# Encoder trunk in three-product float32: the feed-forward low halves made by an accumulating transfer, and the first weights loaded chunk by chunk

## The chip, the cores and the metric

The kernel runs on one core of a Trainium2 chip. The time is device microseconds of one execution; several executions are measured and the median is quoted. Beside the times there is the profile of one execution, taken by the hardware profiler; its span runs from the first instruction to the last.

## The reference

The model is an encoder trunk of two layers on 512 tokens of width 1024, all in float32. Each layer mixes tokens in three ways side by side, merges them, and then applies a SwiGLU feed-forward block and a gated per-layer embedding. Cut to what matters here (the three mixers are attention, a convolution and a windowed attention):

```python
for i in range(DEPTH):                                  # DEPTH = 2
    h = rmsnorm(x, norm_mix[i])
    proj = h @ w_in[i]                                  # 1024 -> 7168
    qa, ka, va, glu_in, qc, kc, vc, gates = jnp.split(proj, SPLITS, axis=-1)
    ...
    x = x + merged @ w_o[i]
    h = rmsnorm(x, norm_ffn[i])
    x = x + (jax.nn.silu(h @ w_ffn_gate[i]) * (h @ w_ffn_up[i])) @ w_ffn_down[i]
    h = rmsnorm(x, norm_ple[i])
    x = x + jax.nn.sigmoid(h @ w_ple_gate[i]) * (p[i] @ w_ple_in[i])
return rmsnorm(x, norm_final)
```

The feed-forward width is 2816, so a layer's gate and up weights are 1024 x 2816 each and its down weights 2816 x 1024.

## The kernel before

**Three products for one.** TensorE takes its operands in a shortened float32 format (`F32R`). To keep float32 accuracy every operand is held as two tiles: a high half, which is the value rounded to that format, and a low half, which is what the rounding left, value minus high half. A product is then three matmuls (`mm3`, lines 175 to 177): high weights by high activations, high weights by low activations, low weights by high activations. The low weights are read by the third matmul of each trio.

**How the two halves are made.** `split` (lines 160 to 162) does it with two engines: ScalarE copies the source into the high tile (an `ACTIVATE` at L141), and VectorE subtracts that from the source into the low tile (a `TENSOR_TENSOR` at L155). `weights` (lines 164 to 171) loads one weight tile and splits it: SyncE's queue loads up to 128x1024 values into a raw tile `wr` (512 KB, L169), and the two halves go to `wh` and `wl`. There are three buffers of each of `wr`, `wh` and `wl`. A raw buffer is free for the next load when VectorE has read it; the two others when TensorE's last matmul on them is done. The last instruction of the split is kept in `self.low`, which one stage outside the feed-forward block uses to place background work behind it.

**Queues and order.** TensorE's order is written out by hand. The other engines' orders are made by a scheduler from priorities; `weights` raises the priority of its instructions so that they are issued early. Each engine works through its own list in order. POOL's list before is short: constants, small memsets, and one `pow` for each norm.

**The feed-forward stage** (`ffn`, lines 917 to 958; instructions named `ffn_...`). A layer does it in two halves of 11 blocks of the feed-forward width. For each block, `gemm` makes the gate product and then the up product, each with one 128x1024 weight tile (24 matmuls). The first gate and up of a layer are done as a `pair` (lines 192 to 202): seven of the eight chunks of both, then the last chunk of both, so both weight tiles are held to the end. After 11 blocks the half of the down projection follows: eight outputs, each with one 128x1024 tile and one 128x384 tile (24 and 9 matmuls). Over two layers that is 120 large tiles and 32 small ones. Beside the weights ScalarE does the SiLU and the high half of the gated result, VectorE the scalings by the norm, the multiplications and the low half.

**The opening** (`opening`, lines 307 to 366; instructions named `pre_...` and the first `glu_...`). The first four blocks of 128 output columns (gate and value of the convolution branch) are made together, chunk by chunk over the eight 128-row chunks of the input, while the input and the weights arrive. Ten warm-up matmuls on zeros (`WARM`, L319) come first. The norm's gains lie in a table of parameters `par`: eight columns of it are loaded first on ScalarE's queue, the rest at the fourth chunk. The weights of the four blocks come as separate transfers of 128, 128, 256 and 512 columns for each block. Each input chunk `x` is scaled and split by `operand` (lines 257 to 266: ScalarE makes the high half, VectorE the low one), and its square is added to a running sum by `sumsq`. A small scale computed from the parameters (`lambdas`, L415) is VectorE work that the scheduler may place between these.

Of the kernel before, what the change touches and what calls it, by code (L numbers as in the profile page):

```python
# [11 lines left out]
F32 = mybir.dt.float32  # L12
F32R = mybir.dt.float32r
I32 = mybir.dt.int32
AF = mybir.ActivationFunctionType
ALU = mybir.AluOpType
# [4 lines left out]
P = 128  # L21
# [5 lines left out]
KD = 8  # L27
HA = 4
HC = 8
CB = 512  # L30
# [11 lines left out]
OFF_QA, OFF_KA, OFF_VA, OFF_GLU = 0, 512, 1024, 1536  # L42
# [2 lines left out]

PAR_L = 8 + 8 + 8 + 1 + 4 + 4 + 4 + 4 * CON3W
PAR = L * PAR_L + 8
WARM = 10
BG = dict(glu=2, natten=1, values=3, diff=1, gatec=2, branchc=2, gateb=4, mergea=4, mergea2=2)
FIRST = (["v"] * 4 + ["pt"] * 2 + ["y", "b"], ["y"] * 5 + ["pt"] * 2 + ["b"])  # L50
EARLY = 6
# [8 lines left out]
class Net:  # L60
# [103 lines left out]
    def weights(self, ap, n):  # L164
        with self.tc.high_priority(offset=min(self.w_ahead, self.tc.cur_priority - self.p0)):
            raw = self.sb("wr", [P, 1024])
            hi = self.sb("wh", [P, 1024], F32R)
            lo = self.sb("wl", [P, 1024], F32R)
            self.nc.sync.dma_start(raw[:, :n], ap[:, :n])  # L169
            self.low = self.split(hi[:, :n], lo[:, :n], raw[:, :n])  # L170
        return hi, lo

    def mm3(self, out, wh, wl, ah, al, first, last):
# [133 lines left out]
    def opening(self):  # L307

        nc, a = self.nc, self.a
        self.parts = self.sb("par", [P, PAR], bufs=1)  # L310
        self.small()
        mix = slice(0, KD)
        xc = [t for _ in range(KD // 2) for t in self.parts_of("x", [512], 2)]
        nc.sync.dma_start(xc[0], a["xT"][0])
        nc.scalar.dma_start(self.parts[:, mix], a["par"][:, mix])
        self.consts()
        warm = self.ps("av")
        for _ in range(WARM):
            nc.tensor.matmul(warm, self.zero_r, self.zero_r[:, None, :].to_broadcast([P, 4, P]),  # L319
                             start=True, stop=True)  # L320
        blocks = []
        lows = [t for _ in range(2) for t in self.parts_of("qk", [1024], 2, F32R)]
        raws = {"t": [self.sb("t", [P, P]) for _ in range(4)],
                "a": [self.sb(t, [P, P]) for t in ("a", "a", "a", "kh")],
                "rp": [self.sb("rp", [P, 256]) for _ in range(4)],
                "e": [self.sb("e", [P, 512]) for _ in range(4)]}
        for m in range(4):
            src = a["w_in"][0, (OFF_GLU + (0 if m % 2 else CB)) // P + m // 2]
            blocks.append((src, self.sb("y", [P, 1024], F32R), lows[m],
                           self.ps("sc" if m == 3 else "mm")))  # L330
        self.first = [b[3] for b in blocks]
        h, st = [], []
        self.i, self.phase = 0, "glu"
        for k in range(KD):
            if k > 1:
                nc.sync.dma_start(xc[k], a["xT"][k])
            pieces = {0: (0, P, "t"), 1: (P, 256, "a"), 2: (256, 512, "rp"), 4: (512, 1024, "e")}
            if k == 0:
                nc.scalar.dma_start(raws["t"][0], blocks[0][0][:, 0:P])
            elif k == 1:  # L340
                nc.scalar.dma_start(xc[1], a["xT"][1])
            elif k == 3:
                nc.scalar.dma_start(self.parts[:, KD:], a["par"][:, KD:])
            h.append(self.operand(xc[k], self.par(0, "mix", k), FIRST[0][k]))
            if k in pieces:
                c0, c1, tag = pieces[k]
                for m, (src, wh, wl, _) in enumerate(blocks):
                    raw = raws[tag][m]
                    if k or m:
                        nc.sync.dma_start(raw, src[:, c0:c1])  # L350
                    if k or m:
                        self.split(wh[:, c0:c1], wl[:, c0:c1], raw)
                    else:
                        nc.vector.tensor_copy(wh[:, c0:c1], raw)
                        self.tt(wl[:, c0:c1], raw, wh[:, c0:c1].bitcast(F32), ALU.subtract)
            s = slice(k * P, k * P + P)
            for src, wh, wl, ps in blocks:
                self.mm3(ps, wh[:, s], wl[:, s], *self.halves(h[k]), k == 0, k == KD - 1)
            if k:
                self.sumsq(k - 1, xc[k - 1], st)  # L360
            if k == KD - 1:
                self.sumsq(k, xc[k], st)
                self.main_norm(st[0], (1, 1), xc)
            self.tick()
        self.p0 = self.tc.cur_priority
        return h
# [785 lines left out]
def _blocks(w):  # L1152
    k, m = w.shape[-2:]
    lead = w.shape[:-2]
    n = len(lead)
    w = w.reshape(*lead, k // P, P, m // P, P)
    w = w.transpose(*range(n), n + 2, n + 1, n, n + 3)
    return np.ascontiguousarray(w).reshape(*lead, m // P, P, (k // P) * P)


def _vblocks(w):
    w = w.reshape(L, KD, P, 2, 256).transpose(0, 3, 2, 1, 4)
    return np.ascontiguousarray(w).reshape(L, 2, P, KD * 256)
# [7 lines left out]
def _cols(v):  # L1171
    v = v.reshape(-1, v.shape[-1])
    return v.reshape(v.shape[0], -1, P).transpose(2, 0, 1).reshape(P, -1)


def _token_order():
    t = np.arange(S)
    return (t % GR) * GW + t // GR


def _rope_tables():
    inv = np.float32(1.0) / (10000.0 ** (np.arange(0, 64, 2) / 64)).astype(np.float32)
    ang = np.arange(S, dtype=np.float32)[:, None] * inv[None, :]
    ang = np.concatenate([ang, ang], axis=-1)
    cos, sin = np.cos(ang), np.sin(ang)
    sin[:, :32] = -sin[:, :32]
    n = _token_order()
    return np.ascontiguousarray(
        np.stack([np.concatenate([c[n].T, c[n].T], axis=0) for c in (cos, sin)])).astype(np.float32)


def _bias_tiles(rpb):
    t = np.arange(S)
    w, r = t // GR, t % GR
    cs = np.clip(w - NA_KC // 2, 0, GW - NA_KC)
    out = np.full((L, HC, 4, P, NW), FILL, dtype=rpb.dtype)
    for qt in range(4):
        q = np.arange(qt * P, (qt + 1) * P)
        k = np.arange(NW) + KEY0[qt]
        ro = r[k][None, :] - r[q][:, None] + NA_KR - 1  # L1200
        co = w[k][None, :] - w[q][:, None] + NA_KC - 1
        ok = (w[k][None, :] >= cs[q][:, None]) & (w[k][None, :] < cs[q][:, None] + NA_KC)
        out[:, :, qt] = np.where(ok, rpb[:, :, np.where(ok, ro, 0), np.where(ok, co, 0)],
                                 out[:, :, qt])
    out = out.reshape(L, HC, 2, 2, P, NW).transpose(0, 1, 2, 4, 3, 5)
    return np.ascontiguousarray(out)


def _layout(v):
    n = _token_order()  # L1210
    f = {k: np.asarray(a) for k, a in v.items()}
    w_in = f["w_in"]
    par = []
    for i in range(L):
        par += [_cols(f["norm_mix"][i]), _cols(f["norm_ffn"][i]), _cols(f["norm_ple"][i]),
                _cols(f["subln_g"][i]), _cols(f["conv_b"][i]), _cols(f["cln_g"][i]),
                _cols(f["cln_b"][i]),
                f["conv_w"][i, :, 0, :].reshape(CON3W, 4, P).transpose(2, 1, 0).reshape(P, -1)]
    par.append(_cols(f["norm_final"]))
    lam = np.stack([np.stack([f["lam_q1"], f["lam_q2"]]), np.stack([f["lam_k1"], f["lam_k2"]])])  # L1220
    down = f["w_ffn_down"].reshape(L, 2, HB * P, D)
    return {
        "xT": np.ascontiguousarray(f["x"][0][n].T).reshape(KD, P, S),
        "pT": np.ascontiguousarray(f["p"][:, 0][:, n].transpose(0, 2, 1)).reshape(L, 2, P, S),
        "par": np.ascontiguousarray(np.concatenate(par, axis=1)),
        "lam": np.ascontiguousarray(np.broadcast_to(lam.reshape(1, 2, 2 * L * 64), (P, 2, 2 * L * 64))),
        "rope": _rope_tables(),
        "bias": _bias_tiles(f["rpb"]),
        "w_in": _blocks(w_in),
        "w_va": _vblocks(w_in[:, :, OFF_VA:OFF_VA + 512]),  # L1230
        "w_vc": _wide(w_in[:, :, OFF_VC:OFF_VC + 512]),
        "w_br_a": _blocks(f["w_br_a"]),
        "w_br_b": _blocks(f["w_br_b"]),
        "w_br_c": _blocks(f["w_br_c"]),
        "w_o": _blocks(f["w_o"]),
        "w_fg": _blocks(f["w_ffn_gate"]),
        "w_fu": _blocks(f["w_ffn_up"]),
        "w_fd": _blocks(down),
        "w_pi": _blocks(f["w_ple_in"]),
        "w_pg": _blocks(f["w_ple_gate"]),  # L1240
    }
# [15 lines left out]
```

## Time and profile before

| | |
|---|---|
| median of 3 runs | 1819.57 us (1818.94 to 1822.36) |
| the profiled execution | 1819.71 us |
| its span | 1817.9 us |
| granted TensorE clock, mean | 0.999 |
| feed-forward weights loaded | 44 + 44 + 32 tiles of 512 KB, 32 of 192 KB |
| feed-forward low halves on VectorE | 152 instructions, 164.7 us |
| transfer engines' share over the span | q1, SyncE's queue: 38.3% |

The page of the profile gives busy time of each engine: PE is TensorE's matmuls, PEld its weight loads, DVE is VectorE, ACT ScalarE, POOL GpSimd, SP SyncE, whose queue only issues transfers (SPq). The chain of waits is the work that ended last, followed back from the end. In the groups a line reads: source line, engine, operation, output tile from input tiles, shapes and count, then busy time and mean duration, then the engine's idle time just before and what ended it. In a timeline the first number is the start in us from the span's start and the second the duration; what stands in square brackets is the idle time before and its releaser. A table of windows gives, for a stretch, each engine's busy us and instructions, the granted TensorE clock, the transfer engines' share and GB/s. A DMA issue line gives the count, the KB of one, and the median us from issue to landing.

### The profile page before, as it was taken

The numbers are of one execution on the slowest core, as the hardware profiler recorded it, in microseconds if no ns is written. First come the engines' busy times: TensorE is split into PE (matmuls) and PEld (weight loads), VectorE is DVE, ScalarE is ACT, GpSimd is POOL, SyncE is SP. The second block draws the span as 40 slices with busy tenths as digits, with TensorE's granted clock in tenths as the row PEclk, the third lists the DMA queues.
The fourth block names the chain that finished last, engine by engine and source line by source line (L and its number), as shares of the span: only waits on it lengthen the run. The fifth ranks groups of instructions, "written<-read, shape, count | busy, mean of one in ns | idle before, by whom it ended". The sixth has DMA issues, their size and how long they took to land.

```text
span 1817.9 us, 23237 instructions
## 1 busy us (share of the span) xinstructions
PE 1806.6 (99%) x8628; PEld 1514.5 (83%) x8628; DVE 1188.2 (65%) x1913; ACT 767.2 (42%) x1316; POOL 24.6 (1%) x58
## 2 busy tenths in 40 slices
PE   9999999999999999999999999999999999999998
PEld 7888888888888888888888888888888888888887
DVE  7877888988644434445777788889875443344456
ACT  5577555325332222233535765552353332232344
POOL 0000000000000000000000000000000000000000
PEclk9999999999999999999999999999999999999999
DMA  5665531325422233223446655322362322322232
GB/s 194 194 180 167 157 110 59 105 96 178 138 93 94 81 107 103 103 76 118 149 139 202 168 159 153 92 76 95 107 205 94 104 93 80 118 93 97 80 113 93
DMA packets 91455, 221.10 MB, mean 122 GB/s; under 512 B 12240, under 2 KB 22352, under 8 KB 91344
## 3 DMA queue, kind: packets, MB, share of 16 engines
q1 hardware_dynamic: 90192, 218.09, 38.3%
q8 instruction: 68, 1.11, 0.3%
q10 hardware_dynamic: 1152, 1.55, 0.2%
q14 instruction: 43, 0.35, 0.1%
HBM read 180.79 MB, written 7.34 MB: 103 GB/s over the span
## 4 chain that ended last, share of the span: by engine, by line
PE 96%; ACT 2%; DVE 1%; DMA 1%; issue 0%; SPq 0%; POOLq 0%; DVEq 0%; ACTq 0%
PE ffn_mm L175 13%; PE ffn_mm L176 13%; PE ffn_mm L177 13%; PE mergea_mm L176 2%; PE mergea_mm L175 2%; PE mergea_mm L177 2%; PE diff_sc L793 2%; PE gatec_mm L175 2%; PE gatec_mm L176 2%; PE gatec_mm L177 2%; PE gateb_mm L176 2%; PE gateb_mm L175 2%; PE wo_mm L175 2%; PE gateb_mm L177 2%; PE wo_mm L176 2%; PE wo_mm L177 2%
## 5 line engine op out<-in xcount | busy, mean ns | idle before, releaser
L141 ACT ACTIVATE ffn_wh<-ffn_wr 128x1024 fp32r<-128x1024 f32 (+1 forms) x152 | 144.0, 949 | 513.9 <-issue 383.2
L175 PE MATMUL ffn_mm<-wo_h,ffn_wh 128*128 128x512 f32 x704 | 274.2, 390 | 0.0
L177 PE MATMUL ffn_mm<-wo_h,ffn_wl 128*128 128x512 f32 x704 | 273.9, 389 | 0.0
L176 PE MATMUL ffn_mm<-wo_h,ffn_wh 128*128 128x512 f32 x704 | 273.9, 389 | 0.0
L155 DVE TENSOR_TENSOR ffn_wl<-ffn_wr,ffn_wh 128x1024 fp32r<-128x1024 f32 (+1 forms) x152 | 164.7, 1085 | 129.6 <-ACT ffn_wh L141 129.6
L158 DVE SCALAR_TENSOR_TENSOR conv_z<-glu_z,pre_par,conv_z 128x512 f32<-128x512 f32 x240 | 179.6, 749 | 3.3
L177 PEld LDWEIGHTS ffn_mm<-wo_h,ffn_wl 128*128 128x128 f32 x704 | 132.1, 188 | 27.7
L175 PEld LDWEIGHTS ffn_mm<-wo_h,ffn_wh 128*128 128x128 f32 x704 | 132.1, 188 | 27.3
L176 PEld LDWEIGHTS ffn_mm<-wo_h,ffn_wh 128*128 128x128 f32 x704 | 132.2, 188 | 27.2
L155 DVE TENSOR_TENSOR ffn_t<-ffn_t,ffn_mm 128x512 f32<-128x512 f32 x44 | 30.2, 687 | 114.8 <-PE ffn_mm L177 114.8
L155 DVE TENSOR_TENSOR ffn_t<-ffn_mm,wo_r 128x512 f32<-128x512 f32 x44 | 30.4, 691 | 110.4 <-PE ffn_mm L177 110.4
L141 ACT ACTIVATE mergea_wh<-mergea_wr 128x1024 fp32r<-128x1024 f32 (+1 forms) x32 | 27.1, 846 | 96.8 <-PE mergea_mm L176 79.6
L175 PE MATMUL ffn_mm<-ffn_z,ffn_wh 128*128 128x512 f32 x160 | 62.2, 389 | 0.0
L176 PE MATMUL ffn_mm<-ffn_z,ffn_wh 128*128 128x512 f32 x160 | 62.2, 389 | 0.0
L177 PE MATMUL ffn_mm<-ffn_z,ffn_wl 128*128 128x512 f32 x160 | 62.2, 389 | 0.0
L175 PE MATMUL ffn_mm<-ffn_y,ffn_wh 128*128 128x512 f32 x160 | 62.2, 389 | 0.0
L176 PE MATMUL ffn_mm<-ffn_y,ffn_wh 128*128 128x512 f32 x160 | 62.2, 389 | 0.0
L177 PE MATMUL ffn_mm<-ffn_y,ffn_wl 128*128 128x512 f32 x160 | 62.2, 389 | 0.0
L141 ACT ACTIVATE diff_a<-diff_sc,diff_s 128x512 f32<-128x512 f32 x32 | 22.0, 686 | 61.3 <-DVE diff_s L884 61.3
L884 DVE TENSOR_REDUCE diff_s<-diff_sc 128x1 f32<-128x512 f32 x64 | 42.1, 685 | 3.9 <-PE diff_sc L793 3.7
L141 ACT ACTIVATE natten_wh<-natten_wr 128x1024 fp32r<-128x1024 f32 x24 | 25.4, 1058 | 41.6 <-issue 15.2
L155 DVE TENSOR_TENSOR wo_x<-wo_x,ffn_mm 128x512 f32<-128x512 f32 x32 | 22.0, 687 | 31.5 <-PE ffn_mm L177 31.5
(662 smaller groups left out, 4564.9 us busy)
## 6 DMA issues: line engine op xcount, KB each, us to landing
ffn_wr<-w_fg SPq DMA_DIRECT2D x44, 512.0 KB, 3.2
ffn_wr<-w_fu SPq DMA_DIRECT2D x44, 512.0 KB, 3.2
ffn_wr<-w_fd SPq DMA_DIRECT2D x32, 512.0 KB, 3.5
natten_wr<-w_in SPq DMA_DIRECT2D x16, 512.0 KB, 3.6
natten_b<-bias SPq DMA_DIRECT2D x32, 256.0 KB, 3.6
diff_wr<-w_in SPq DMA_DIRECT2D x16, 512.0 KB, 3.8
gatec_wr<-w_in SPq DMA_DIRECT2D x16, 512.0 KB, 3.6
gateb_wr<-w_in SPq DMA_DIRECT2D x16, 512.0 KB, 3.2
```

The source lines that it names most:

```text
L141: i = self.nc.scalar.activation(out, in_, func, **kw)
L155: return self.nc.vector.tensor_tensor(out, a, b, op)
L158: return self.nc.vector.scalar_tensor_tensor(out, a, s, b, op0, op1)
L175: mm(out, wh, ah, start=first, stop=False)
L176: mm(out, wh, al, start=False, stop=False)
L177: mm(out, wl, ah, start=False, stop=last)
L793: self.nc.tensor.matmul(out, st4[:, u, qs], st[:, ks], start=n == 0, stop=n == 1)
L884: nc.vector.tensor_reduce(out=m[:, u:u + 1], in_=sc, op=ALU.max, axis=AX.X, negate=True)
```

## The change

In the feed-forward stage the low half of a weight tile is no longer made by VectorE. ScalarE writes the high half as before and then the negative of the rounded source into the low tile (a second `ACTIVATE`, with scale -1 into an `F32R` tile); then a transfer issued by GpSimd reads the raw tile and adds it onto the low tile, SBUF to SBUF. All other stages keep `split`.

In the opening the host lays the weights of the first four blocks out chunk by chunk (`w_0`: for each 128-row chunk, the 512 columns of the four blocks side by side), and puts the eight norm gains and the first block's first 128 columns into one array `head`. `head` is loaded first on SyncE's queue, the first chunk of x on ScalarE's; then for each chunk one x and one weight transfer of 256 KB on SyncE's queue, and the whole parameter table after the fourth chunk. Each chunk's weights are split in one piece (the first 128 columns of the first chunk by VectorE alone). `WARM` goes from 10 to 8.

```diff
-WARM = 10
+WARM = 8
...
             self.nc.sync.dma_start(raw[:, :n], ap[:, :n])
-            self.low = self.split(hi[:, :n], lo[:, :n], raw[:, :n])
+            if self.phase == "ffn":
+                self.act(hi[:, :n], raw[:, :n], AF.Copy)
+                self.act(lo[:, :n], raw[:, :n], AF.Copy, scale=-1.0)
+                self.low = self.nc.gpsimd.dma_start(lo[:, :n].bitcast(F32), raw[:, :n], accum_op=ALU.add)
+            else:
+                self.low = self.split(hi[:, :n], lo[:, :n], raw[:, :n])
...
-        nc.sync.dma_start(xc[0], a["xT"][0])
-        nc.scalar.dma_start(self.parts[:, mix], a["par"][:, mix])
+        raws = [self.sb(tag, [P, 512]) for tag in ("rp", "e") for _ in range(4)]
+        head = self.sb("a", [P, KD + P])
+        nc.sync.dma_start(head, a["head"])
+        nc.scalar.dma_start(xc[0], a["xT"][0])
+        nc.sync.dma_start(raws[0], a["w_0"][0])
...
         for k in range(KD):
-            if k > 1:
+            if k:
                 nc.sync.dma_start(xc[k], a["xT"][k])
...
+                nc.sync.dma_start(raws[k], a["w_0"][k])
+            if k == 3:
+                nc.sync.dma_start(self.parts, a["par"])
+            hi, lo = his[k], los[k]
             if k == 0:
...
-            h.append(self.operand(xc[k], self.par(0, "mix", k), FIRST[0][k]))
...
+                first = head[:, KD:]
+                nc.vector.tensor_copy(hi[:, :P], first)
+                self.tt(lo[:, :P], first, hi[:, :P].bitcast(F32), ALU.subtract)
+            h.append(self.operand(xc[k], head[:, k:k + 1], FIRST[0][k]))
+            c = slice(0 if k else P, 512)
+            self.split(hi[:, c], lo[:, c], raws[k][:, c])
+            ah, al = self.halves(h[k])
+            for m, ps in enumerate(self.first):
+                s = slice(m * P, m * P + P)
+                self.mm3(ps, hi[:, s], lo[:, s], ah, al, k == 0, k == KD - 1)
...
+def _first(w):
+
+    c = [OFF_GLU + (0 if m % 2 else CB) + m // 2 * P for m in range(4)]
+    w = np.concatenate([w[:, o:o + P] for o in c], axis=1)
+    return np.ascontiguousarray(w).reshape(KD, P, 4 * P)
...
+        "head": np.ascontiguousarray(np.concatenate([_cols(f["norm_mix"][0]), w_0[0, :, :P]], axis=1)),
+        "w_0": w_0,
```

More of the change, by code (lines that the diff above doesn't have):

```diff
@@ L311, in opening @@
         self.small()
-        mix = slice(0, KD)
         xc = [t for _ in range(KD // 2) for t in self.parts_of("x", [512], 2)]
-        nc.sync.dma_start(xc[0], a["xT"][0])
-        nc.scalar.dma_start(self.parts[:, mix], a["par"][:, mix])
+        raws = [self.sb(tag, [P, 512]) for tag in ("rp", "e") for _ in range(4)]
[3 more added lines that the diff above has]
+        nc.sync.dma_start(raws[0], a["w_0"][0])
         self.consts()
@@ L320, in opening @@
                              start=True, stop=True)
[L321 to L331, printed above, removed]
+        his = [t[:, o:o + 512] for t in [self.sb("y", [P, 1024], F32R) for _ in range(4)]
+               for o in (0, 512)]
+        los = [t[:, o:o + 512] for _ in range(2) for t in self.parts_of("qk", [1024], 2, F32R)
+               for o in (0, 512)]
+        self.first = [self.ps(tag) for tag in ("mm", "mm", "mm", "sc")]
         h, st = [], []
@@ L334, in opening @@
         for k in range(KD):
-            if k > 1:
+            if k:
                 nc.sync.dma_start(xc[k], a["xT"][k])
-            pieces = {0: (0, P, "t"), 1: (P, 256, "a"), 2: (256, 512, "rp"), 4: (512, 1024, "e")}
+                nc.sync.dma_start(raws[k], a["w_0"][k])
+            if k == 3:
+                nc.sync.dma_start(self.parts, a["par"])
+            hi, lo = his[k], los[k]
             if k == 0:
[L339 to L343, printed above, removed]
-            h.append(self.operand(xc[k], self.par(0, "mix", k), FIRST[0][k]))
[L345 to L358, printed above, removed]
+                first = head[:, KD:]
[8 more added lines that the diff above has]
+                self.mm3(ps, hi[:, s], lo[:, s], ah, al, k == 0, k == KD - 1)
             if k:
@@ L1220, in _layout @@
     lam = np.stack([np.stack([f["lam_q1"], f["lam_q2"]]), np.stack([f["lam_k1"], f["lam_k2"]])])
+    w_0 = _first(w_in[0])
     down = f["w_ffn_down"].reshape(L, 2, HB * P, D)
```

## The prediction

> **What bounds the kernel now.** I read the page first (busy shares), then what TensorE waited for, then the feed-forward stage in order of time on ScalarE and VectorE, then the DMA issues.
>
> ```profile
> span 1817.9 us, 23237 instructions
> PE 1806.6 (99%) x8628; PEld 1514.5 (83%) x8628; DVE 1188.2 (65%) x1913; ACT 767.2 (42%) x1316; POOL 24.6 (1%) x58
> ...
> PE 96%; ACT 2%; DVE 1%; DMA 1%; issue 0%; SPq 0%; POOLq 0%; DVEq 0%; ACTq 0%
> ```
>
> TensorE is busy for all but 11.3 us of the span and is 96% of the chain of waits. VectorE at 65% decides nothing on average, so taking work from it buys only what TensorE waits for it. These are all such waits:
>
> ```profile
> PE pre_mm L176 <- DVE glu_v L158: 1.7, 1, 1.7
> PE pre_av L319 <- DVE pre_zeror L388: 1.1, 1, 1.1
> PE natten_tr L718 <- ACT natten_e L141: 0.9, 2, 0.4
> PE diff_mm L597 <- ACT diff_rp L141: 0.6, 2, 0.3
> PE natten_tr L718 <- DVE natten_a L155: 0.4, 2, 0.2
> ```
>
> None lies in the feed-forward stage. So the half of the change that stands there can gain nothing on TensorE and can only lose; the half at the start has 1.7 us before it. The rhythm of the feed-forward stage (ScalarE, VectorE and SyncE rows of a stretch of gate and up blocks, then ScalarE in the down projection):
>
> ```profile
> 560.34 1.06 ACT L141 ACTIVATE ffn_wh<-ffn_wr 128x1024 fp32r<-128x1024 f32 x1 [3.86 <-issue]
> 561.44 1.23 DVE L155 TENSOR_TENSOR ffn_wl<-ffn_wr,ffn_wh 128x1024 fp32r<-128x1024 f32 x1 [0.23 <-ACT ffn_wh L141]
> 562.69 0.33 SPq L169 DMA_DIRECT2D ffn_wr<-w_fg  x1
> 565.78 1.06 ACT L141 ACTIVATE ffn_wh<-ffn_wr 128x1024 fp32r<-128x1024 f32 x1 [3.86 <-issue]
> ...
> 627.66 1.06 ACT L141 ACTIVATE ffn_wh<-ffn_wr 128x1024 fp32r<-128x1024 f32 x1 [1.51 <-PE ffn_mm L176]
> 633.05 0.53 ACT L141 ACTIVATE ffn_wh<-ffn_wr 128x384 fp32r<-128x384 f32 x1 [4.33 <-PE ffn_mm L176]
> 635.09 1.06 ACT L141 ACTIVATE ffn_wh<-ffn_wr 128x1024 fp32r<-128x1024 f32 x1 [1.51 <-PE ffn_mm L176]
> ```
>
> A 128x1024 weight tile costs TensorE 565.78 - 560.34 = 5.44 us, a 128x384 tile about 2.03 us (635.09 - 627.66 less 5.40). ScalarE copies the next tile as soon as a buffer comes free; there are three of each kind, so a tile is prepared while TensorE works through the two before it. That distance is the cover for everything added.
>
> **The change part by part.**
>
> *Removed:* 152 VectorE subtractions (1.23 us for 1024 columns, 0.56 for 384). Gain: none, no TensorE wait ends there.
>
> *Added on ScalarE:* 152 negating copies, 1.06 or 0.53 us like the copy before them, 120 x 1.06 + 32 x 0.53 = 144 us, about 1.1 us more per 5.44 us tile on an engine with 3.86 us free in each. The SiLU behind it comes 1.06 us later; the first of a layer has two new copies before it (2.1 us), and the accumulator bank that it helps to free is wanted some 2 to 3 us after it was free. I cost this at nothing, and at up to 1 us per layer if that cover is gone.
>
> *Added on the POOL queue:* 152 accumulating transfers, SBUF to SBUF. Each waits for the negating copy; behind it in POOL's order stands only the next one, and once per layer the `pow` of the norm (1.01 us), which isn't due until several tiles' work later. Each transfer is waited for by the third matmul of its tile (0.45 us after the first), and by SP's load of the next tile into the same raw buffer.
>
> How late may it land? Call D the time from the end of the negating copy to landing.
> - Gate and up: the copy starts at 560.34, the tile's first low half is read two tiles later, 560.1 + 10.88 + 0.45 = 571.4. Two copies end at 562.5. D may be 9.0.
> - Down projection (tiles of 1024 and 384 in turn): a large tile has one large and one small before it: 627.45 + 5.44 + 2.03 + 0.45 = 635.4, the copies end at 629.8: D may be 5.55. A small one: 640.8 - 634.1 = 6.7, for 192 KB.
> - Once per layer the first gate and up pair holds two buffers until its end (about 10.2 us after the stage begins); the tile that gets the first of them is read at 16.8 and copied by 12.6: D may be 4.2.
>
> The raw buffer has room: in gate and up a load after a landing at the last moment, 571.4, ends 3.5 us later at 574.9, and ScalarE wants it three tiles after 560.34, at 576.7; in the down projection it is about as close.
>
> What is D? Before has no transfer on the POOL queue and none that accumulates, so I bound it by the loads:
>
> ```profile
> ffn_wr<-w_fg SPq DMA_DIRECT2D x44, 512.0 KB, 3.2
> ffn_wr<-w_fd SPq DMA_DIRECT2D x32, 512.0 KB, 3.5
> ffn_wr<-w_fd SPq DMA_DIRECT2D x32, 192.0 KB, 2.3
> ...
> 505.00:595.00 90.00, 90.00 (x403) 74.54 (x401) 42.66 (x52) 28.63 (x36) 1.01 (x1) 1.00 0.28 94
> ```
>
> From below: a plain load of the size, 3.2 us; all is then covered. From above: every byte crosses three times (raw read, negative read, sum written) and the transfer engines fill up. A load takes 0.28 x 5.44 = 1.5 us of all 16 engines; three times that beside the load is 6.0 of each 5.44 us, more than there is, and D grows past 9. Between them: the two down rows give (3.5 - 2.3) / 320 KB, so 1.9 us of 512 KB scale with bytes and 1.6 are fixed. An accumulate reads two streams where a load reads one: 1.6 + 2 x 1.9 = 5.4. The next load starts when the previous transfer has landed, so it runs beside this one and takes a share, 0 to 1.5 us; issue by POOL's software is not in any row. I take 5.4 + 0.9 = 6.3 us, an estimate, nearer to the lower rows than to saturation, with 3.2 and 10 as the ends.
>
> The Trainium skill (DMA: Bandwidth & Descriptors, "Anatomy of one DMA — SWDGE (gpsimd) path") fits a GpSimd transfer as 2.0 us plus bytes over 436 GB/s: 3.2 us for 512 KB once, an estimate of 4.4 us with two reads; no run here shows it yet, and by it the whole sum for the feed-forward stage would be 2 x 0.2 = 0.4 us. Collectives: The Full Stack, "The bandwidth ceiling: the fold count and why AG ≠ RS ≠ AR", says that an adding transfer is halved by its two source reads, not by the addition; by it the factor of two above stands.
>
> The sum at D = 6.3: per layer once 6.3 - 4.2 = 2.1, twice 4.2. In the down projection a late large tile loses 6.3 - 5.55 = 0.75; that wait gives the next pair the same slack, so every second large tile is late: 8 of them in each of 4 halves, 4 to 5 late, 18 x 0.75 = 13.5. Gate and up: nothing. Together +17.7 us.
>
> *The opening.* Before, VectorE sits 1.96 us for the parameter load, with a small scale (L415) ahead of the fourth chunk's low half, and TensorE waits 1.67 us:
>
> ```profile
> 14.76 0.15 DVE L415 TENSOR_SCALAR glu_subg<-pre_par 128x1 f32<-128x1 f32 x1 [1.96 <-DMA pre_par<-par]
> 15.64 0.50 PE L176 MATMUL pre_mm<-glu_v,pre_y 128*128 128x512 f32 x1 [1.67 <-DVE glu_v L158]
> ```
>
> Afterwards that scale stands behind the eighth chunk on VectorE, so the wait goes: -1.67. Two warm-up matmuls fewer (0.43 us each) let the first product start up to 0.75 us earlier; but blocks 2 to 4 of the first chunk now hang on one 256 KB transfer issued behind 69 KB and beside 256 KB of x. At the 238 to 290 GB/s of the first microseconds, 581 KB from 2 us on land at about 4.3, with some 1 us of completion 5.3; 0.53 us of copy later TensorE may go on at about 6.1, where block 2 starts now (6.06). So +0.2. Each later chunk needs 512 KB per 2.72 us of products, 190 GB/s, and 2.0 us of ScalarE and 2.1 of VectorE: covered. SP's queue holds 17 issues of about 0.4 us in place of the old order; parameters go through it after the fourth chunk, wanted only after the eighth. Sum -1.5, ends -2.4 (both savings) and +1.5 (first chunk late, or the TensorE clock not yet up after 8 warm-ups).
>
> Total: +17.7 - 1.5 = +16.2. The profiled execution took 1819.71 us (1817.9 span and 1.8 around it), 0.14 above the median of 1819.57: 1835.8, so 1836.
>
> **The rivals.** A run of this kernel varies by about 0.2% (1818.94 to 1822.36), so I call less than that no change.
> - *Hidden after all* (not slower): D stays under 5.5. Then only the pair's tile is late (2 x 0 to 1.3) and the opening gains 1.5: 1818 to 1821. For it: the 3.2 us row and transfer engines only 28% busy. Against it: two reads and a load beside them put 5.5 at the edge. 0.27. (The Trainium skill's fit, cited above, leads here.)
> - *Faster by over 0.2%*: hidden, and both savings of the opening (2.4) come with the 1.9 us of attention waits in the list above, less work on VectorE or not: 1819.6 - 4.3 = 1815. Only if small waits far from the change go as well. 0.06.
> - *The transfers set the pace* (slower, more than forecast): D of 10 us. Gate and up lose 10 - 9.0 per three tiles, 29 x 1.0; down 18 x 4.45 = 80; the pairs 10: +118, 1937. Saturation alone, 6.0 against 5.44 us per tile over 2 x 338 us of stage, costs 70, about 1888. For it: the third crossing; against it: reads and writes may overlap. 0.25.
> - *The accumulating transfers are late in the down projection alone* (the forecast, D of 5.7 to 9.2): 1822 to 1890. 0.42.
>
> **How the numbers follow.** The time is that of the last case at its middle. Faster 0.06; same 0.27; slower 0.42 + 0.25 = 0.67. Range 1817 to 1900: it leaves out the faster case and the part of the pace case above D of 9.3, about 2 in 10 together. The forecast case's own range is 1822 to 1890.
>
> **What would show it.** Landing times of the accumulating transfers: above 5.5 and below 9 us for 512 KB confirms the mechanism. TensorE waits for `ffn_wl` from a DMA, of 0.5 to 2 us, at every second large tile of the down projection and once after each first pair, none in gate and up. The wait at 15.6 us gone, TensorE's first product no later than 5.4. It is wrong if no such TensorE wait appears, if gate and up tiles take more than 5.44 us, or if the transfer engines' share in the stage passes 0.9.

## The result, and the profile after

| | before | after |
|---|---|---|
| median of the runs made together | 1819.63 us (1818.94 to 1822.36) | 1845.95 us (1843.59 to 1848.94) |
| ratio | | 1.0144, 95% interval 1.0132 to 1.0156 |
| the profiled execution, its span | 1819.71 us, 1817.9 us | 1843.59 us, 1841.8 us |

The changed kernel is slower by 26.3 us. The forecast was 1836, with a range of 1817 to 1900. First the page of the kernel after: span, busy time and the chain of waits by engine.

```profile
span 1841.8 us, 23549 instructions
...
PE 1812.7 (98%) x8626; PEld 1512.1 (82%) x8626; DVE 1031.7 (56%) x1754; ACT 893.1 (48%) x1461; POOL 157.5 (9%) x210
...
PE 82%; DMA 7%; issue 4%; ACT 3%; DVE 2%; POOL 0%; POOLq 0%; SPq 0%; DVEq 0%; ACTq 0%
```

VectorE lost 156.5 us of work and the time did not fall for it. Transfers, 1% of the chain before, are now 7% of it. Next what TensorE waited for (total us, times, longest).

```profile
PE ffn_mm L182 <- DMA ffn_wl<-ffn_wr: 19.0, 18, 2.4
PE pre_av L326 <- DVE pre_zeror L382: 1.1, 1, 1.1
```

The wait of 1.7 us in the opening is gone, and a new one heads the list: the third matmul of a trio waits for the accumulating transfer. The stages, from the start of TensorE's first to the start of its last product in the two traces (the opening with its warm-ups, gate and up without the first pair), say where that is:

| stage (the four down and gate/up values: layer 1, both halves, then layer 2) | before, us | after, us |
|---|---|---|
| opening and first four blocks | 27.94 | 26.11 |
| gate and up | 108.70, 119.45, 108.70, 119.45 | 108.72, 120.28, 108.72, 120.38 |
| down projection | 59.61 four times | 65.89, 65.69, 66.59, 64.09 |

The down projection lost 23.8 us, gate and up 1.8 (at the first tiles behind a down projection, where the waits run on), and all stages between the opening and the first feed-forward block start 1.98 us earlier. That is +23.6 of the 23.9 us between the spans. The transfers, by issue (count, KB, median us to landing) and by queue (packets, MB, share of the 16 transfer engines):

```profile
q1 hardware_dynamic: 89472, 218.39, 38.7%
q0 software_dynamic: 21888, 69.22, 20.4%
...
ffn_wl<-ffn_wr POOLq DMA_DIRECT2D x120, 512.0 KB, 5.9
ffn_wr<-w_fg SPq DMA_DIRECT2D x44, 512.0 KB, 4.4
...
ffn_wr<-w_fd SPq DMA_DIRECT2D x32, 512.0 KB, 4.7
```

GpSimd's queue (q0) moves a third of what SyncE's (q1) moves and takes over half as much engine time. The loads themselves became slower: 3.2 to 4.4 us and 3.5 to 4.7. One stall, from the chain of waits in the first down projection (start, duration, what):

```profile
632.48 3.99 DMA ffn_wl<-ffn_wr
...
636.53 6.43 DMA ffn_wr<-w_fd
...
644.03 1.05 ACT ffn_wl L141
645.08 0.40 issue
645.48 7.09 DMA ffn_wl<-ffn_wr
...
652.61 0.50 PE ffn_mm L182
```

It reads as a round. A small tile's accumulating transfer lands at 636.47 and so frees a raw tile; the load into that tile starts at 636.53 and takes 6.43 us; ScalarE makes its two copies; the large accumulating transfer takes 7.09 us; TensorE, which could have gone on at 650.80, goes on at 652.61. Not every stall is like this one: at 23 of the 32 large tiles of the down projection the copies did not wait for a raw tile.

Two things could set such a stall. *Distance*, the prediction's mechanism: the copies are made as soon as TensorE releases the high and low tiles, and a transfer of this length is too long behind that. *The raw buffer*: SyncE's load must now wait for the transfer's landing, where before it waited only for VectorE, so the copies themselves start late. The prediction had said of the second that there is room, if less in the down projection. The experiments are made to tell these apart.

### The profile page after: what moved, and what is told of

It is laid out like the page before. It is cut to its first block, busy times and chain, and to the rows that moved or that the text cites. A ratio compares the mean times of both kernels' runs of the same rounds, so it can differ in the third digit from the quotient of the medians.

```text
span 1841.8 us, 23549 instructions
## 1 busy us (share of the span) xinstructions
PE 1812.7 (98%) x8626; PEld 1512.1 (82%) x8626; DVE 1031.7 (56%) x1754; ACT 893.1 (48%) x1461; POOL 157.5 (9%) x210
## 3 DMA queue, kind: packets, MB, share of 16 engines
q0 software_dynamic: 21888, 69.22, 20.4%
## 4 chain that ended last, share of the span: by engine, by line
PE 82%; DMA 7%; issue 4%; ACT 3%; DVE 2%; POOL 0%; POOLq 0%; SPq 0%; DVEq 0%; ACTq 0%
PE ffn_mm L182 10%; PE ffn_mm L180 9%; PE ffn_mm L181 9%; DMA ffn_wl<-ffn_wr 5%; PE mergea_mm L182 2%; PE mergea_mm L181 2%; PE mergea_mm L180 2%; PE diff_sc L787 2%; PE gatec_mm L180 2%; PE gatec_mm L181 2%; PE gatec_mm L182 2%; PE gateb_mm L182 2%; PE gateb_mm L181 2%; PE gateb_mm L180 2%; PE wo_mm L182 2%
## 5 line engine op out<-in xcount | busy, mean ns | idle before, releaser
L173 POOL DMA_DIRECT2D ffn_wl<-ffn_wr x152 | 132.2, 870 | 747.8 <-ACT ffn_wl L141 722.4
L141 ACT ACTIVATE ffn_wl<-ffn_wr 128x1024 fp32r<-128x1024 f32 (+1 forms) x152 | 141.2, 929 | 0.0
L155 DVE TENSOR_TENSOR ffn_t<-ffn_t,wo_r 128x512 f32<-128x512 f32 x44 | 30.4, 692 | 64.3 <-ACT ffn_t L141 64.3
L182 PEld LDWEIGHTS ffn_mm<-ffn_z,ffn_wl 128*128 128x128 f32 x160 | 30.0, 187 | 32.0 <-DMA ffn_wl<-ffn_wr 26.3
```

What stands on the lines that cost most here:

```text
L141: i = self.nc.scalar.activation(out, in_, func, **kw)
L155: return self.nc.vector.tensor_tensor(out, a, b, op)
L173: self.low = self.nc.gpsimd.dma_start(lo[:, :n].bitcast(F32), raw[:, :n], accum_op=ALU.add)
L182: mm(out, wl, ah, start=False, stop=last)
```

## The experiments

Each row is against runs of the kernel before on the same chip (medians 1819.8 to 1820.2 us).

| run | time, us | ratio and 95% interval |
|---|---|---|
| new opening alone | 1817.88 | 0.9987 (0.9979 to 0.9996) |
| new feed-forward stage alone | 1847.72 | 1.0157 (1.0143 to 1.0171) |
| old kernel, parameters later | 1818.47 | 0.9990 (0.9981 to 0.9999) |
| new opening, ten warm-ups | 1818.11 | 0.9991 (0.9982 to 0.9999) |
| own raw tiles for small weights | 1820.57 | 1.0005 (0.9995 to 1.0014) |
| copies swapped in the source | 1846.23 | 1.0143 (1.0128 to 1.0158) |
| no feed-forward loads | 1817.81 | 0.9989 (0.9979 to 0.9999) |
| copying instead of adding | 1820.51 | 1.0002 (0.9992 to 1.0011) |
| copies swapped and held so | 1836.50 | 1.0092 (1.0077 to 1.0107) |
| own high and low tiles for small weights | 1850.34 | 1.0174 (1.0159 to 1.0190) |
| accumulating in gate and up alone | 1818.15 | 0.9990 (0.9981 to 1.0000) |
| large transfers in two parts | 1834.97 | 1.0085 (1.0068 to 1.0102) |

The kernels that lose time vary more from run to run: the last one, in two parts, from 1829.66 to 1837.80 us over four runs, and its profile is of the fastest. The loss of the feed-forward stage is counted below from 1817.88, the run with the new opening alone: the changed kernel's is 1845.95 - 1817.88 = 28.1 us.

### The two parts apart

New opening alone: `weights` of the changed kernel without its new branch, so all stages use `split`.

> New opening, feed-forward halves split by ScalarE and VectorE as before. If the two parts of the change are independent: the opening shortened the profiled execution by 2.0 us (every stage between it and the feed-forward stage starts 1.98 us earlier after the change), so 1817.6 us against 1819.6, and the four down-projection halves are back at 59.61 us, the gate and up halves at 108.70 and 119.45. If TensorE gives the gain back at a later wait that the old feed-forward stage would show: 1818.5 to 1819.6.

New feed-forward stage alone: the kernel before with the new branch in `weights`.

> Old opening, feed-forward low halves by the accumulating transfer. If the parts are independent: the loss of the stage, 23.8 us in the down projection and some 1.7 in gate and up, plus up to 1 us of jitter, on top of the old time: 1845 to 1848 us, ratio 1.014 to 1.0155. If the loss depended on where the opening left the buffers: outside of that, and the four down-projection halves differ from 65.9, 65.7, 66.6 and 64.1 us by over 1 us each.

Measured 1817.88 us, all stages from gate and up on at their old lengths, and 1847.72 us. Its four down halves (63.65, 68.33, 65.45, 65.30 us) differ from the changed kernel's by 1 to 3 us each, but so do those of a further run of the changed program itself, below (67.07, 66.75, 65.18, 65.49); the sum, 262.7 us, is that of the changed kernel, 262.3. Which tiles are late varies from one execution to the next, the loss hardly. The parts are independent as far as these runs can tell: -2.0 us and +27.8 us.

### Where the opening's 2 us come from

```diff
-            elif k == 3:
+            elif k == 6:
                 nc.scalar.dma_start(self.parts[:, KD:], a["par"][:, KD:])
```

> The kernel before with one edit: the rest of the parameter table is loaded at the seventh chunk of x instead of the fourth, which puts the small scale that waits for it behind the last low half in VectorE's order. If the 1.67 us wait came from that order alone: the wait at 15.6 us goes and the time falls by 1.6 to 1.7 us to 1817.9. If the fourth chunk's low half was late by itself (its weights or x): the wait stays at over 1 us and the time within 0.5 us of before.

```diff
-WARM = 8
+WARM = 10
```

> As the first of these runs (new opening, old feed-forward stage), with ten warm-up matmuls as before in place of eight. If the fewer warm-ups bring their 0.75 us (the prediction's upper end): 1818.3 us. If what sets the start is the arrival of the first 256 KB of weights (the second block's products start at 6.22 us after the change, 6.06 before): the first product moves from 4.6 to about 5.4 us but the second block stays at 6.2, and the time is 1817.6 within 0.3.

The first, one number changed in the old kernel, shortens the opening from 27.94 to 26.00 us; the new opening has 26.09, and 26.01 with ten warm-ups. The times (1818.47, 1817.88, 1818.11) can't be told apart. So the gain is the wait for the parameter load that the small scale had held in VectorE's order, and neither the new weight layout nor the fewer warm-ups bring anything more. Why the warm-ups don't, TensorE's rows show (start, duration), of the new opening with eight and then with ten:

```profile
1.05 3.78 PE L326 MATMUL pre_av<-pre_zeror 128*128 128x512 f32 x8 [1.05 <-DVE pre_zeror L382]
4.64 0.80 PE L180 MATMUL pre_mm<-glu_v,pre_y 128*128 128x512 f32 x1
5.42 0.70 PE L181 MATMUL pre_mm<-glu_v,pre_y 128*128 128x512 f32 x1
...
6.18 0.39 PE L180 MATMUL pre_mm<-glu_v,pre_y 128*128 128x512 f32 x1
```

```profile
1.05 4.57 PE L326 MATMUL pre_av<-pre_zeror 128*128 128x512 f32 x10 [1.05 <-DVE pre_zeror L382]
5.45 0.39 PE L180 MATMUL pre_mm<-glu_v,pre_y 128*128 128x512 f32 x1
...
6.13 0.39 PE L180 MATMUL pre_mm<-glu_v,pre_y 128*128 128x512 f32 x1
```

The first product starts 0.81 us earlier with eight, but the first two products then take 0.80 and 0.70 us instead of 0.39, and the second block starts at 6.18 against 6.13. The expectation was right about the second block; it had put this down to the weights' arrival, and the long products were not in it.

### What the transfer costs, and beside what

Without the loads of the stage (the one tile is loaded in `ffn`, ahead of its loop):

```diff
-            self.nc.sync.dma_start(raw[:, :n], ap[:, :n])
+            if self.phase != "ffn":
+                self.nc.sync.dma_start(raw[:, :n], ap[:, :n])
```

> The changed kernel without the loads of the feed-forward weights: one tile is loaded at the start of the stage of each layer and every weight tile is made from it (both copies and the accumulating transfer stay). If the landing is long because each transfer runs beside a load: it falls from 5.9 us to 3 to 4.5 us for 512 KB, no wait is left in the stage, 1817 to 1818.5 us. If it is long by itself (issue and descriptors of GpSimd's queue, two reads): it stays over 5.5 us and the loss over 6 us, 1824 us or more.

Copying instead of adding:

```diff
-                self.low = self.nc.gpsimd.dma_start(lo[:, :n].bitcast(F32), raw[:, :n], accum_op=ALU.add)
+                self.low = self.nc.gpsimd.dma_start(lo[:, :n].bitcast(F32), raw[:, :n])
```

> The changed kernel with the transfer copying the raw tile onto the low tile instead of adding it (the low tiles then hold the raw values). Same queue, same bytes written, same waits, one read fewer. If the second read is the price (the prediction took 1.9 us for 512 KB): the landing falls from 5.9 to 4 to 4.6 us, the transfer takes as much engine time as a load, and the loss to under 3 us, 1817 to 1821 us. If GpSimd's queue is the price and the addition free: landings over 5.5 us and 1835 us or more.

The issue row of the run without loads:

```profile
ffn_wl<-ffn_wr POOLq DMA_DIRECT2D x120, 512.0 KB, 4.4
```

And of the run that copies, its queue, GpSimd's instruction (busy us, mean ns) and the issue row:

```profile
q0 software_dynamic: 19328, 69.22, 9.4%
...
L173 POOL DMA_DIRECT2D ffn_wl<-ffn_wr x152 | 81.6, 537 | 774.2 <-ACT ffn_wl L141 758.8
...
ffn_wl<-ffn_wr POOLq DMA_DIRECT2D x120, 512.0 KB, 2.9
```

Without loads the transfer lands in 4.4 us, no wait is left in the stage, and the time is that of the new opening alone. So the transfer is not too long by itself. VectorE's work is the same here as in the changed kernel (1032.1 and 1031.7 us), so that is not what makes it longer there. By the fit of the Trainium skill (DMA: Bandwidth & Descriptors, "Anatomy of one DMA — SWDGE (gpsimd) path"), two reads of 512 KB come to an estimate of 4.4 us; this run agrees, and what a load beside it does is not in that fit. The plain copy of the same 69.22 MB takes 9.4% of 1818.9 us, 171 us of all 16 engines, and the adding transfer 20.4% of 1841.8, 376 us: 2.2 times as much. It lands in a median of 2.9 us (4.0 at the large tiles of the down projection, where the adding one took 6.9), and the loss is 2.6 us, with the raw tiles shared as they were. A short transfer therefore has room in the round of the raw buffer; the round alone, without the long transfer, is no bound.

### Distance or raw buffer

Own raw tiles for the small weights (the four `rp` tiles are idle in this stage):

```diff
-            raw = self.sb("wr", [P, 1024])
+            raw = self.sb("rp", [P, 512]) if self.phase == "ffn" and n < 1024 else self.sb("wr", [P, 1024])
```

> The changed kernel, but the 384-column raw tiles of the down projection have four buffers of their own, so a load of 1024 columns waits for the accumulating transfer of the third large tile before it (22 us earlier) and not of the third tile of any size (11 us). If the loss is the distance alone (the time from the end of the negating copy to the landing, against the 5.55 us that the tile order allows): at landings of 6.4 to 6.9 us it stays at 16 to 26 us, 1834 to 1844 us. If the loss is the raw buffer (a load that waits for the transfer before it, so the copies start late): under 8 us are left, 1818 to 1826, and ScalarE's waits for ffn_wr go.

1820.57 us: 2.7 us of loss in place of 28.1, as the raw buffer predicts, though nothing was taken from the transfer, and the high and low tiles come free as before. TensorE's wait:

```profile
PE ffn_mm L182 <- DMA ffn_wl<-ffn_wr: 1.0, 2, 0.7
```

But the landings fell too, from a median of 6.93 us to 4.97 for the large tiles of the down projection. In the changed kernel a raw tile comes free, and its load starts, just as the next large transfer starts; here the load is well under way by then. There a load starts between 1 us before and 1.2 us after 25 of the 32 large transfers of the down projection; these landed in a median of 7.1 us, the 7 others in 4.4. Here it is so at 11 of 32, with a median of 5.6; the 21 others landed in 4.75, with a load beside them for a median of 3.7 us. SyncE's and GpSimd's rows, of the changed kernel and then of this run:

```profile
645.48 0.88 POOL L173 DMA_DIRECT2D ffn_wl<-ffn_wr  x1 [2.58 <-ACT ffn_wl L141]
...
646.02 0.33 SPq L169 DMA_DIRECT2D ffn_wr<-w_fd  x1
```

```profile
633.75 0.33 SPq L169 DMA_DIRECT2D ffn_wr<-w_fd  x1
...
636.31 0.86 POOL L173 DMA_DIRECT2D ffn_wl<-ffn_wr  x1 [2.23 <-ACT ffn_wl L141]
```

So the run shows that sharing the raw tiles is needed for the loss. The landings speak for transfers made longer by a load at the wrong moment, but the run alone does not part that from late copies. The next three runs take the distance from the other side.

Copies swapped, so that the transfer starts one copy earlier. Swapping the two lines in the source did nothing:

> The changed kernel with ScalarE's two copies in the other order: the negating one first, so each accumulating transfer may start 1.06 us earlier. If the loss is the distance: each of the 18 late tiles gains up to 1.06 us, and since a late tile gives the next pair slack, 2 to 6 us of loss are left, 1820 to 1824 us. If the transfer engines themselves set the pace (their share is 0.81 in the stage): an earlier start is queued away, 1840 us or more.

ScalarE's rows show the high copy still ahead of the negating one (the scheduler put it there), so this was the changed kernel again: 1846.23 us, against 1845.95. Then with the order held:

```diff
-                self.act(hi[:, :n], raw[:, :n], AF.Copy)
-                self.act(lo[:, :n], raw[:, :n], AF.Copy, scale=-1.0)
+                neg = self.act(lo[:, :n], raw[:, :n], AF.Copy, scale=-1.0)
+                high = self.act(hi[:, :n], raw[:, :n], AF.Copy)
+                self.tc.add_manual_dep(high.ins, neg.ins.name, ...)
```

> The changed kernel with the negating copy ahead of the high copy, held in that order by an ordering dependency, so that each accumulating transfer of 1024 columns starts 1.06 us earlier. If the loss is the distance from the negating copy to the read alone: 2 to 6 us of loss are left, 1820 to 1824 us. If it is the round of the raw buffer (landing, next load 4.6 to 6.4 us, copies, transfer 6.8 to 7.1 us): that round gets 1.06 us shorter for a large tile, about 8 rounds in each of 4 down-projection halves of which some 4 were late, so the loss falls by 10 to 20 us to 1824 to 1834. If transfers and loads only collide the more: 1840 us or more.

1836.50 us: 18.6 us of loss are left. That is neither theory's figure, 9.5 us gained and not 20 or more, just short of what the round gives.

```diff
-            hi = self.sb("wh", [P, 1024], F32R)
-            lo = self.sb("wl", [P, 1024], F32R)
+            if self.phase == "ffn" and n < 1024:
+                hi, lo = self.sb("rp", [P, 512], F32R), self.sb("e", [P, 512], F32R)
+            else:
+                hi = self.sb("wh", [P, 1024], F32R)
+                lo = self.sb("wl", [P, 1024], F32R)
```

> The changed kernel with high and low tiles of their own (four of each) for the 384-column weights of the down projection; the raw tiles stay shared, three for all. The copies of a large tile then need not wait until TensorE is through with the third tile before it, but only the third large tile. If the loss is the distance (copies held back by TensorE's release, D too long behind it): it goes, under 4 us left, 1818 to 1822 us. If the loss is the raw buffer, whose next load waits for the landing: releasing the copies earlier does not free the raw tiles earlier than the transfers land, so over 12 us stay, 1830 us or more.

1850.34 us, and the reading is spoilt by a wait that neither theory had:

```profile
PE ffn_mm L183 <- ACT ffn_pt L141: 16.6, 4, 5.0
PE ffn_mm L185 <- DMA ffn_wl<-ffn_wr: 5.3, 4, 1.6
```

```profile
ACT ffn_rp L141 <- DMA ffn_wr<-w_fd: 164.1, 32, 6.9
```

With more tiles free, weight copies stand further ahead in ScalarE's order, and the last gated block of each half (`ffn_pt`), which the first small tile's products need, comes behind them: four waits, 16.6 us. What holds those copies is the raw tile: ScalarE waits for its load ahead of each of the 32 small tiles, the last row, and mostly comes to the next pair of tiles after 8.6 us, where TensorE needs 7.47. So the round of the raw tiles sets the pace of the copies once the high and low tiles do not. Around each of the four waits, 3.3 to 5.0 us long in the trace, the granted clock was 0.50 for 3.4 to 6.8 us, which adds to the loss. The stalls on the transfer fell to 5.3 us, but since the stage had 16.6 us of idle time for catching up, this run decides nothing on distance.

```diff
-                self.low = self.nc.gpsimd.dma_start(lo[:, :n].bitcast(F32), raw[:, :n], accum_op=ALU.add)
+                for c in ((slice(0, 512), slice(512, n)) if n > 512 else (slice(0, n),)):
+                    self.low = self.nc.gpsimd.dma_start(lo[:, c].bitcast(F32), raw[:, c], accum_op=ALU.add)
```

> The changed kernel with each accumulating transfer of 1024 columns issued as two of 512, one after the other; TensorE waits for the second only at its fifth trio, 2.7 us after the first. Raw, high and low tiles, copies and the bytes moved are the same, and a raw tile comes free no earlier. If the loss is the distance (a transfer landing 7.3 us after the copies where 5.45 are allowed): the first half lands 1.5 us or more before the whole did and the second has 2.7 us more room, so under 8 us of loss are left, 1818 to 1826 us. If the loss is the raw buffer's round: it stays or grows by the second issue (0.86 us), 1842 us or more.

1834.97 us: 17.1 us left. Again between: relieving the distance takes away 11 us, not 20. What is left shows in TensorE's wait, and then in ScalarE's waits for loaded raw tiles (total us, times, longest):

```profile
PE ffn_mm L183 <- DMA ffn_wl<-ffn_wr: 8.1, 9, 1.2
```

```profile
ACT ffn_wh L141 <- DMA ffn_wr<-w_fd: 29.4, 15, 3.6
...
ACT ffn_wh L141 <- DMA ffn_wr<-w_fg: 22.1, 9, 4.3
...
ACT ffn_wh L141 <- DMA ffn_wr<-w_fu: 17.7, 4, 6.2
```

In the changed kernel these three sum to 20.7 us over 11 waits; here to 69.2 over 28. With the distance out of the way, the copies wait for the raw tile instead. At 17 of the 32 large tiles of the down projection the copy starts within 0.2 us of the raw tile's landing, and they hold all but 0.1 of the 9 us that TensorE stalls at large tiles; the 15 whose copies were on time hold next to nothing, though their second parts land 7.1 us (median) after the copies. Both theories hold, one behind the other.

### Gate and up alone

```diff
-            if self.phase == "ffn":
+            if self.phase == "ffn" and not self.down:
```

> The changed kernel with the accumulating transfer in the gate and up products alone; the down projection splits with VectorE as before. If the gate and up blocks can carry it (their two halves lost 0.0 and 0.9 us in the profiled execution, and the 0.9 at the first tile after the down projection): the down halves are back at 59.61, gate and up at 108.7 and 119.5, 1817.9 us within 0.5, as the run with the new opening alone. If the 0.9 is theirs: 1819 to 1820.

1818.15 us, halves of 108.74, 119.45, 108.73, 119.45 us, with 88 accumulating transfers of 6.0 us. Where TensorE gives a tile 5.44 us every time, the transfer is fully hidden; the 0.9 us per layer there had run over from the down projection.

## Why the prediction was right, and by how much it was off

*No gain from VectorE.* Right: 156.5 us less work, and with all waits of the stage gone (the run without loads) the time is that of the new opening alone.

*ScalarE's copies, SiLU and GpSimd's `pow` at nothing.* Right: in the run without loads and with the transfers in gate and up alone every half has its old length, with these costs still in it.

*The mechanism: late accumulating transfers at every second large tile of the down projection, none in gate and up.* Right in place, and near in number: 16 of the 18 waits on the transfer stand at the 32 large tiles there, where 18 were forecast; the two others, 1.1 us together, are at gate and up's first tile behind a down projection. The term was mis-sized, 18 x 0.75 = 13.5 us against 23.8, by its size D:

| large tile of the down projection | predicted, us | measured, us |
|---|---|---|
| transfer with nothing beside it, from the end of the copies | 5.4 | 4.82 (0.40 to issue, 4.42 to landing) |
| share of the load beside it | 0.9 | 2.5 |
| D | 6.3 | 7.33 |
| D that is allowed | 5.55 | 5.90 |
| late by (D less what is allowed) | 0.75 | 1.43 |

The measured values are medians over the 32 tiles, from ScalarE's, GpSimd's and TensorE's rows; the 4.42 is from the run without loads, the 2.5 the difference to 7.33, and the 5.90 is the time from the copies' end to the first low product where nothing waited (in the run with raw tiles of their own, 5.45 to the tile's first product and 0.45 on). The 16 late tiles stalled TensorE for 1.3 us in the mean.

The transfer itself was dearer in the estimate than on the chip. The step that failed is the 0.9 us for its share with the next load, which "starts when the previous transfer has landed, so it runs beside this one". That was seen, but only as a share of the bytes. Within gate and up of the changed kernel, transfers that ran beside loads for 2 to 3.5 us landed in a median of 5.0, for over 5 us in 6.4; in the down projection the latter took 7.1. A longer transfer also has more time for a load beside it, so these figures alone do not say which made which; the run without loads does.

*"The raw buffer has room ... in the down projection it is about as close."* The second weak step. Three raw tiles serve large and small weights in turn, so each carries one large and one small tile in three pairs, 3 x 7.47 = 22.4 us. Before, that took 3.5 + 2.3 of loads and 2.3 + 1.1 of ScalarE's and VectorE's work, 9.2 us. After, 4.7 + 2.3 of loads, 2.0 + 1.0 of copies, 0.4 twice and landings of 6.9 and 3.5: 21.2 us, before any wait for TensorE's release. At 9 of the 32 large tiles the copy started within 0.2 us of the raw tile's landing; these hold 4.2 of the 21.0 us of stalls at large tiles, and the 23 whose copies were on time hold 16.8. So in the changed kernel itself most stalls are distance, as predicted, with a D of 7.5 (median of those 23); that sharing the raw tiles lies behind such a D is shown by the run with raw tiles of their own, and that the round is the next bound by the run in two parts. By which share it lengthens the transfers and by which it delays the copies stays open.

*The pair's tile, 2 x 2.1 us.* Wrong: no wait. Its transfer took 4.89 us from the copies' end, with no load beside it, and 5.03 were allowed, not 4.2.

*The opening, -1.5.* Right in kind: the wait went (-1.67), the stage is 1.83 us shorter, the runs show -1.4 to -2.0. The second block starts at 6.22 us for 6.06 (+0.16, predicted +0.2); the stages behind start 1.98 us earlier. The savings of the warm-ups, in the range's lower end, do not exist.

*The rivals.* Hidden after all: it holds as soon as the transfer is shorter or the load is out of its way (four runs at 1817.8 to 1820.6). Transfers setting the pace: no, the engines' share in gate and up is 0.82, from 0.28, and the tile still takes 5.44 us; the estimate of three crossings at full price was too high, measured is 2.2 times a plain copy. Its sum is off a little besides: 29 + 80 + 10 is 119 and not 118, and the pairs, at 2 x (10 - 4.2), would be 11.6. By the same terms the forecast's upper end, a D of 9.2, comes to about 1900 and not 1890.

The errors, +10.3 in the down projection, +1.8 after it, -4.2 at the pairs and -0.5 in the opening, make 7.4 of the 7.8 us between forecast and profiled execution; the median of the runs lies another 2.4 us higher.

No version beats the kernel before by more than about 0.1%: the new opening alone, 1817.88 us, and the old kernel with the parameters loaded later, 1818.47, gain that much, and their intervals only just leave out no change.

## What to carry to other kernels

A transfer that takes the place of an instruction holds its source until it lands, so the staging buffer's round grows by the whole landing time, and the next load then starts at the same moment as the next transfer. Add up that round (loads, copies, landings against the time the buffers allow) and price each transfer with the load that will run beside it, not alone. Look at the smallest tile that the same buffers serve: what was free at 5.44 us for each tile cost 28 us where every second tile gives only 2.03. And before a layout is rebuilt for a wait, see which instruction in the waiting engine's order holds it: here one number moved the parameter load and brought all that the new opening brings.

## What the runs showed of the hardware

An accumulating transfer of 512 KB within SBUF, issued by GpSimd, landed in a median of 4.42 us with no load beside it, in medians of 5.0 to 7.1 us with one, the longest when the load started at about the same moment; a plain copy on the same queue, loads running, in a median of 2.9. The adding one costs 2.2 times the engine time of the plain one (the Trainium skill, Collectives: The Full Stack, "The bandwidth ceiling: the fold count and why AG ≠ RS ≠ AR", gives a factor of 1.93 for an adding transfer in a collective, put down to its two source reads; 2.2 is a little more), and GpSimd's instruction 0.87 us instead of 0.54.

With eight warm-up matmuls TensorE's first two products took 0.80 and 0.70 us, with ten 0.39, at a granted clock of 1.00 in both; the products came at full pace, 0.23 us apart, from 5.96 us with eight and from 5.45 with ten. The warm-ups stood 0.43 us apart, as products did in the run with high and low tiles of their own at a granted clock of 0.50. Why is not shown. In that run the granted clock fell to 0.50 around TensorE waits of 3.3 to 5.0 us; the waits of the changed kernel in this stage, 2.4 us at most, left it at 1.00.
